# One inference step of a hybrid decoder on one core: store of new keys and values, pace of the sample group's keys, copies of new columns, scaling of the prompt's weights

## The chip, the cores and the metric

The kernel runs on one core of one Trainium2 chip. The metric is the device time of one execution in microseconds; the time before is 831.85 us, the median of three runs (829.95 to 833.71). Engines are named as in the profile: PE is the matmul engine, PEld its weight loads, DVE the vector engine, ACT the scalar engine, POOL the GpSimd engine, SP the engine whose queue issues most of the DMAs.

## The reference

One decoder layer with fp32 inputs is computed for two groups that share the weights: a prompt of 512 tokens, and a sample group of 8 sequences with 8 new tokens each and a cache of 1024 past keys and values. In outline:

```
h    = rmsnorm(x);  proj = h @ w_in                  # 1024 -> 3584 columns
rq, rk, rv, rg, aq, ak, av = split(proj)             # seven sections of 512: 8 heads x 64
ro   = silu(rg) * groupnorm(retention(rq, rk, rv))   # chunks of 128, recurrent state
ao   = dilated_attention(aq, concat(cache_k, ak), concat(cache_v, av))
                                                     # windows (128,1), (512,4), (2048,16), ALiBi
x    = x + concat(ro, ao) @ w_out
ua, ub = split(rmsnorm(x) @ w_up)
x    = x + (silu(conv3(ua)) * ub) @ w_down
y    = rmsnorm(x)
```

Outputs are y, the retention states, the windows of keys and values (the cache with the new rows behind it) and the last rows of the convolution, for both groups.

## The kernel before, in words

The 576 tokens lie along the free axis, the 128 columns of a weight chunk on the partitions. Every large product runs as three matmuls of split operands (high by high, high by low, low by high) over two halves of 288 tokens; the six matmuls for one block of 128 rows are one dense step (`dense`, L245 to L261). A chunk of `w_in` is eight steps. ACT and DVE split each chunk into its two parts (L219, L229), SP loads the chunks three deep (L211).

The work is written as Python generators, "streams", and a planner (`Merge`, L96 to L143) decides while the kernel is built in which order their instructions are emitted; on the chip each engine then runs its instructions in that order. A stream yields a cost, a delay before it may go on, and if wanted a third number, its charge (otherwise the cost is charged). Streams without a declared total (post-processing, a unit of attention) go first as soon as their delay is over. Among those with a total (`in_proj` 130,000 ns, `attn_prompt` 32,700, `attn_sample` 59,600) the one with the smallest sum of charge / what is left goes next. A stream that yields None is stuck until another moves on, and its sum is then lifted to the smallest of the others. `room(n)` sticks a stream while fewer than n of four PSUM tiles are free.

Heads are taken in pairs, hp 0 to 3. The input projection takes the three retention sections of each pair first, then for each pair the sections 5 (attention keys), 4 (queries) and 6 (values), then the gates. From pair 2 on it waits until `used` of the pair two before is 6: four prompt units and two sample units have done their value matmuls (L579). `in_post` (L521) scales the projected rows; for sections 5 and 6 it transposes them to token rows (`natural`, L489) and `store_window` (L501) writes them out: the prompt's 512 rows in one DMA, the sample group's 64 rows in eight, one for each sequence.

The prompt's attention runs in units of 128 queries (`attn_unit`, L741): score matmuls, penalties and minimum on DVE (L773), exponential on ACT (L780), reciprocal of the sums on DVE (L783), scaling of the weights of both heads on POOL (L785), then transposes on PE (L791), copies out of PSUM, and the value matmuls (L804).

The sample group's attention (`attn_sample`, L850) has eight units: pair hp and half g of the eight sequences. For each of a unit's four sequences x, `keys` (L870) transposes 768 gathered cache rows on PE (L877) and copies them into a key tile `kt` (L878; five buffers); then the loads of later keys and values are issued (L861, L863). When the four key tiles are there and the projection has given the pair's queries, new keys and new values, four POOL copies put the eight new key columns behind each tile's 768 (L977), and the unit itself is started: score matmuls (L887; columns 0 to 511, then 512 to 775), softmax (L894 to L904), transposes (L910), value matmuls (L923), transposes of the result (L938). At most two units are under way. After the first retention pass the three streams, projection, prompt and sample group, run side by side from 150 us on; the output projection follows at about 341 us, then the feed-forward part.

Of the kernel before, what the change touches and what calls it, by code (L numbers as in the profile page):

```python
# [14 lines left out]
OP = mybir.AluOpType  # L15
# [5 lines left out]
NP = 512  # L21
NS = 64
T = NP + NS
H2 = T // 2
B = 8
TS = 8
PAST = 1024
# [5 lines left out]
KEYS = 768  # L33
# [113 lines left out]
def decoder_step(ctx, tc, a):  # L147
    nc = tc.nc
    pe, dve, act, pool, sp = nc.tensor, nc.vector, nc.scalar, nc.gpsimd, nc.sync
# [7 lines left out]
    def mtile():  # L157
        return psm[0].tile([P, 512], F32, name="m", tag="m")
# [3 lines left out]
    def room(n):  # L162

        while held[0] + n > 4:
            yield None
        held[0] += n

    def give(n):
        held[0] -= n
# [4 lines left out]
    def f32(ap):  # L174
        return ap.bitcast(F32)
# [149 lines left out]
    def halves():  # L325
        return [(h2, slice(h2 * 64, h2 * 64 + 64)) for h2 in range(2)]
# [155 lines left out]
    for i in range(2):  # L482
        t = atp.tile([P, B, 32], F32, name=f"qb{i}", bufs=1)
# [17 lines left out]
    def store_window(nat, which, hp):  # L501
        c = slice(hp * P, (hp + 1) * P)
        op_ = a[f"o_w{which}_p"].rearrange("a (j p) h d -> p (a j) (h d)", p=P)[:, :, c]
        sp.dma_start(op_, nat[:, 0:4])
        os_ = a[f"o_w{which}_s"]
        for b in range(B):
            sp.dma_start(os_[b, PAST:PAST + TS].rearrange("t h d -> t (h d)")[:, c], nat[b * TS:(b + 1) * TS, 4])

    copies = []
    for which in "kv":  # L510
# [9 lines left out]
    R, A, ready, ret_done = {}, {}, set(), [0]  # L520
    def in_post(m, ps):  # L521
# [30 lines left out]
        else:  # L552
# [16 lines left out]
            if sec > 4:  # L569
                yield 0.0, 3100.0  # L570
                store_window(n, "k" if sec == 5 else "v", hp)
# [22 lines left out]
    for lst, shape, nme in ((sbds, [P, 3, P], "sbd"), (s0s, [P, B, P], "s0"), (qms, [P, B, NS], "qm")):  # L594
        t = rp.tile(shape, F32, name=nme, bufs=1)
# [4 lines left out]
    for i in range(2):  # L600
        t = rp.tile([P, 4, 10], F32, name=f"gst{i}", bufs=1)
# [134 lines left out]
    def load_bias(hp):  # L736
        for h2 in range(2):
            pbs[2 * hp + h2] = atp.tile([P, 512], F32, name="pb", tag="pb", bufs=2)
            sp.dma_start(pbs[2 * hp + h2], a["c_pbias"][2 * hp + h2])

    def attn_unit(hp, i):  # L741

        n = (i + 1) * P
        S, PT = [], []
        if i:

            q_ = A[hp][4][:, i * P:(i + 1) * P]
            qa = [kvb[0].tile([P, P], F32R, name=f"qa{h2}", tag=f"qa{h2}", bufs=2) for h2 in range(2)]
            ql = kvb[0].tile([P, P], F32R, name="ql", tag="ql", bufs=2)
            for h2, q in halves():  # L750
                act.copy(qa[h2][q], q_[q])
                act.copy(qa[h2][other(h2)], q_[q])
            yield 0.0, 1000.0
            for h2, q in halves():
                dve.tensor_sub(ql[q], q_[q], f32(qa[h2][q]))
            yield 0.0, 500.0
        yield from room(2)
        pss = [mtile() for _ in halves()]
        if i == 0:
            for h2, q in halves():  # L760
                pe.matmul(pss[h2][:, :n], A[hp][4][q, :P], A[hp][5][q, :n], start=True, stop=True)
        else:
            for h2 in range(2):
                pe.matmul(pss[h2][:, :n], qa[h2], kk[hp][h2][:, :n], start=True, stop=False)  # L764
            for h2, q in halves():
                pe.matmul(pss[h2][:, :n], ql[q], kk[hp][h2][q, :n], start=False, stop=True)  # L766
        for ps in pss:
            S.append((ps, atp.tile([P, 512], F32, name="s", tag="s", bufs=4),
                      atp.tile([P, 4], F32, name="sc", tag="sc", bufs=8)))
        scored[hp] = scored.get(hp, 0) + 1  # L770
        yield 2 * (i + 1) * 110.0, 100.0
        for h2, (ps, s, c) in enumerate(S):
            dve.tensor_tensor_reduce(out=s[:, :n], in0=ps[:, :n], in1=pbs[2 * hp + h2][:, 512 - n:], scale=1.0,  # L773
                                     scalar=3e38, op0=OP.add, op1=OP.min, accum_out=c[:, 0:1])
        give(2)
        if i == 3 and hp < 3:
            load_bias(hp + 1)
        yield 0.0, n + 300.0
        for ps, s, c in S:
            act.activation(s[:, :n], s[:, :n], AF.Exp, bias=c[:, 0:1], scale=-1.0, accum_out=c[:, 1:2])  # L780
        yield 0.0, 600.0
        for ps, s, c in S:
            dve.reciprocal(c[:, 2:3], c[:, 1:2])  # L783
        for ps, s, c in S:
            pool.tensor_scalar(s[:, :n], s[:, :n], c[:, 2:3], 1.0, op0=OP.mult, op1=OP.mult)  # L785
        yield 0.0, 2.5 * n + 300.0
        yield from room(2)
        for ps, s, c in S:
            ps = mtile()
            for j in range(i + 1):  # L790
                pe.transpose(ps[:, j * P:(j + 1) * P], s[:, j * P:(j + 1) * P], ident)  # L791
            PT.append((ps, atp.tile([P, 4, P], F32, name="pt", tag="pt", bufs=3)))
        yield 2 * (i + 1) * 110.0, 100.0
        for h2, (ps, pt) in enumerate(PT):
            (dve.tensor_copy if h2 else act.copy)(pt[:, :i + 1].rearrange("p j q -> p (j q)"), ps[:, :n])
        give(2)
        yield 0.0, n + 400.0
        if hp not in O:
            yield from room(1)
            O[hp] = [mtile(), 0]  # L800
        o_ps = O[hp][0]
        for j in range(i + 1):
            for h2, q in halves():
                pe.matmul(o_ps[q, i * P:(i + 1) * P], A[hp]["v"][:, j, q], PT[h2][1][:, j], start=j == 0, stop=j == i)  # L804
        yield (i + 1) * 230.0, 100.0
        used[hp] = used.get(hp, 0) + 1
        O[hp][1] += 1
        if O[hp][1] == 4:
            act.copy(aoT[:, hp, :NP], o_ps)
            give(1)  # L810
            half[hp] = half.get(hp, 0) + 1
            if half[hp] == 3:
                ready.add(4 + hp)
        flying["p"] -= 1
# [15 lines left out]
    def other(h2):  # L830
        return slice(64 - h2 * 64, 128 - h2 * 64)

    def attn_prompt():
        load_bias(0)
        for hp in range(4):
            while not (hp in A and all(x in A[hp] for x in (4, 5, 6))) or not kvb or hp and scored.get(hp - 1) != 4:
                yield None
            yield from k_split(hp)
            for i in range(4):
                while flying["p"] > 1:  # L840
                    yield None
                flying["p"] += 1
                mg.add(attn_unit(hp, i))
                yield 0.0, 2500.0, 2 * (i + 1) * 430.0
# [5 lines left out]
    def attn_sample():  # L850
        K, V, KT, SB = {}, {}, {}, {}
        units = [(hp, g) for hp in range(4) for g in range(2)]
# [17 lines left out]
        def keys(u, x):  # L870
            hp, g = units[u]
            b = 4 * g + x
            kt = kvb[0].tile([P, SK], F32, name="kt", tag="kt", bufs=5)
            for w in range(2):
                ps = mtile()
                for j in range(3):
                    pe.transpose(ps[:, j * P:(j + 1) * P], K[u, x][:, 3 * w + j], ident)  # L877
                (act.copy if w else dve.tensor_copy)(kt[:, w * 384:w * 384 + 384], ps[:, :384])  # L878
            del K[u, x]
            KT[u, x] = kt  # L880

        def unit(u):
            hp, g = units[u]
# [66 lines left out]
        def ahead(n, which):  # L950
            while loaded[which] < min(n, 32):
                u, x = divmod(loaded[which], 4)
                (K if which == "k" else V)[u, x] = load(u, x, which)
                loaded[which] += 1
# [7 lines left out]
        for u in range(8):  # L962
            hp, g = units[u]
            for x in range(4):
                yield from room(2)
                keys(u, x)
                give(2)
                yield 660.0, 1600.0
                ahead(4 * u + x + 4, "k")
                while len(V) > 5:  # L970
                    yield None
                ahead(4 * u + x + 1, "v")
            while not (hp in A and all(y in A[hp] for y in (4, 5, 6))) or flying["s"] > 1:
                yield None
            for x in range(4):
                b = 4 * g + x
                pool.tensor_copy(KT[u, x][:, KEYS:], A[hp][5][:, NP + b * TS:NP + (b + 1) * TS])  # L977
            flying["s"] += 1
            mg.add(unit(u), None, 600.0)
            yield 0.0, 1000.0, 4100.0  # L980

    last_in = []
    mg.add(in_proj(), 130.0e3)
# [6 lines left out]

    mg.add(ret_all())
    mg.add(attn_sample(), 59.6e3)
    mg.run(lambda: len(evac) == 3)
    psxx.close()
# [101 lines left out]
    for i in range(2):  # L1096
        u = fp.tile([P, UE], F32, name=f"ue{i}")
# [226 lines left out]
```

## Time and profile before

| | us |
|---|---|
| median of three runs (lowest, highest) | 831.85 (829.95, 833.71) |
| the profiled execution | 832.6 |
| its span, first to last instruction | 830.8 |
| PE busy | 813.8 |
| DVE busy | 412.5 |
| ACT busy | 295.3 |
| POOL busy | 148.0 |

The span is shorter than the execution's time, since start and end of the program lie outside of it. Matmuls are pipelined and their ends are modelled, so a busy PE can still be slower than its best. The granted clock is the share of full speed that PE's clock had.

### The profile page before, as it was taken

The numbers are of one execution on the slowest core, as the hardware profiler recorded it, in microseconds if no ns is written. First come the engines' busy times: TensorE is split into PE (matmuls) and PEld (weight loads), VectorE is DVE, ScalarE is ACT, GpSimd is POOL, SyncE is SP. The second block draws the span as 40 slices with busy tenths as digits, with TensorE's granted clock in tenths as the row PEclk, the third lists the DMA queues.
The fourth block names the chain that finished last, engine by engine and source line by source line (L and its number), as shares of the span: only waits on it lengthen the run. The fifth ranks groups of instructions, "written<-read, shape, count | busy, mean of one in ns | idle before, by whom it ended". The sixth has DMA issues, their size and how long they took to land.

```text
span 830.8 us, 15970 instructions
## 1 busy us (share of the span) xinstructions
PE 813.8 (98%) x6559; PEld 772.2 (93%) x6559; DVE 412.5 (50%) x792; ACT 295.3 (36%) x511; POOL 148.0 (18%) x234
## 2 busy tenths in 40 slices
PE   7999999999999999999999999999999999999995
PEld 6999999887887888999999999999999999999995
DVE  4664555665546456754545455432235545453333
ACT  5422232554446367333223323311223323342222
POOL 1321202011111113023122212100012322210111
PEclk9999999999999999999999999999999999999998
DMA  9354653658787774455265554543334445543213
GB/s 269 102 173 125 203 175 97 185 158 236 217 219 197 219 212 121 110 177 179 78 201 178 178 174 125 168 140 89 93 102 153 152 152 178 171 156 96 71 52 115
DMA packets 180247, 128.68 MB, mean 155 GB/s; under 512 B 15424, under 2 KB 176848, under 8 KB 179661
## 3 DMA queue, kind: packets, MB, share of 16 engines
q1 hardware_dynamic: 179021, 93.75, 40.3%
q10 hardware_dynamic: 928, 33.63, 11.2%
q8 instruction: 52, 0.85, 0.4%
q0 software_dynamic: 224, 0.28, 0.1%
q14 instruction: 22, 0.18, 0.1%
HBM read 121.52 MB, written 39.66 MB: 194 GB/s over the span
## 4 chain that ended last, share of the span: by engine, by line
PE 96%; ACT 1%; DVE 1%; DMA 0%; POOL 0%; issue 0%; ACTq 0%; DVEq 0%; POOLq 0%
PE d L254 75%; PE m L877 2%; PE m L923 2%; PE d L451 2%; PE m L804 1%; PE d L887 1%; PE m L791 1%; PE m L495 1%; PE px L410 1%; PE m L1214 1%; PE px L254 1%; PE m L663 1%; PE m L764 1%; PE d L910 1%; PE m L766 1%; PE m L627 1%
## 5 line engine op out<-in xcount | busy, mean ns | idle before, releaser
L219 ACT ACTIVATE whi<-wraw 128x1024 fp32r<-128x1024 f32 (+2 forms) x114 | 110.6, 970 | 364.9 <-issue 182.6
L229 DVE TENSOR_TENSOR wlo<-wraw,whi 128x1024 fp32r<-128x1024 f32 (+2 forms) x114 | 126.7, 1112 | 120.4 <-ACT whi L219 117.0
L254 PE MATMUL d<-bhi,whi 128*128 128x288 f32 x768 | 173.3, 307 | 0.0
L254 PE MATMUL d<-bhi,wlo 128*128 128x288 f32 x768 | 164.3, 295 | 0.0
L254 PE MATMUL d<-blo,whi 128*128 128x288 f32 x768 | 163.9, 295 | 0.0
L254 PE MATMUL d<-hhi,whi 128*128 128x288 f32 x704 | 150.9, 296 | 0.0
L254 PE MATMUL d<-hhi,wlo 128*128 128x288 f32 x704 | 150.8, 296 | 0.0
L254 PE MATMUL d<-hlo,whi 128*128 128x288 f32 x704 | 150.7, 296 | 0.0
L254 PEld LDWEIGHTS d<-bhi,whi 128*128 128x128 f32 x768 | 121.5, 189 | 5.2 <-issue 3.6
L254 PEld LDWEIGHTS d<-bhi,wlo 128*128 128x128 f32 x768 | 123.3, 188 | 0.0
L254 PEld LDWEIGHTS d<-blo,whi 128*128 128x128 f32 x768 | 123.2, 188 | 0.0
L254 PEld LDWEIGHTS d<-hhi,whi 128*128 128x128 f32 x704 | 113.4, 189 | 0.1
L254 PEld LDWEIGHTS d<-hhi,wlo 128*128 128x128 f32 x704 | 113.4, 189 | 0.0
L254 PEld LDWEIGHTS d<-hlo,whi 128*128 128x128 f32 x704 | 113.4, 189 | 0.0
L1122 DVE TENSOR_TENSOR ue<-d,rstd_b 128x512 f32<-128x512 f32 x22 | 15.2, 691 | 74.6 <-PE d L254 74.6
L1141 POOL TENSOR_TENSOR g<-g,cv 128x512 f32<-128x512 f32 x20 | 25.7, 1287 | 142.1 <-DVE g L1138 136.7
L785 POOL TENSOR_SCALAR s<-s,sc 128x128 f32<-128x128 f32 (+3 forms) x32 | 18.2, 575 | 141.1 <-DVE sc L783 139.9
L1038 POOL TENSOR_TENSOR acc<-acc,sq 128x576 f32<-128x576 f32 x13 | 20.9, 1607 | 104.2 <-ACT sq L1037 104.2
L1127 POOL COPY cout<-ue 128x2 f32<-128x2 f32 x22 | 5.7, 258 | 137.8 <-DVE ue L1122 137.8
L878 DVE COPY kt<-m 128x384 f32<-128x384 f32 x32 | 17.8, 556 | 22.4 <-PE m L877 21.2
L878 ACT COPY kt<-m 128x384 f32<-128x384 f32 x32 | 15.3, 477 | 38.4 <-PE m L877 36.8
L877 PE MATMUL m<-ident,kc 128*128 128x128 f32 x192 | 27.2, 277 | 0.9 <-ACT spt L916 0.9
(264 smaller groups left out, 1030.7 us busy)
## 6 DMA issues: line engine op xcount, KB each, us to landing
wraw<-in_w_up_dram SPq DMA_DIRECT2D x44, 512.0 KB
wraw<-in_w_in_dram SPq DMA_DIRECT2D x26, 512.0 KB
kc<-in_cache_win_k_dram SPq DMA_DIRECT2D x32, 256.0 KB
vc<-in_cache_win_v_dram SPq DMA_DIRECT2D x32, 256.0 KB
wraw<-in_w_down_dram SPq DMA_DIRECT2D x16, 384.0 KB
wraw<-in_w_down_dram SPq DMA_DIRECT2D x16, 320.0 KB
kc<-in_cache_win_k_dram SPq DMA_DIRECT2D x64, 64.0 KB
vc<-in_cache_win_v_dram SPq DMA_DIRECT2D x64, 64.0 KB
```

The lines of the kernel that those rows point to most:

```text
L219: act.activation(split[i][0][:, c], raw[i][:, c], AF.Copy)
L229: dve.tensor_sub(lo[:, c], raw[i][:, c], f32(hi[:, c]))
L254: pe.matmul(ps[:, C0 + s * H2:C0 + (s + 1) * H2], wt[:, rows[k] if rows else k - k0], x[k][:, s * H2:(s + 1) * H2], start=first and k == k ...
L410: pe.transpose(ps[:, s], xn[:r, j, k * P:(k + 1) * P], ident[:r, :r])
L451: pe.matmul(ps[i][:, C0 + s * H2:C0 + (s + 1) * H2], wt[:, k], x[k][:, s * H2:(s + 1) * H2], start=k == 0 and wt is hi and x is xhis, stop ...
L785: pool.tensor_scalar(s[:, :n], s[:, :n], c[:, 2:3], 1.0, op0=OP.mult, op1=OP.mult)
L877: pe.transpose(ps[:, j * P:(j + 1) * P], K[u, x][:, 3 * w + j], ident)
L878: (act.copy if w else dve.tensor_copy)(kt[:, w * 384:w * 384 + 384], ps[:, :384])
L923: pe.matmul(ps[x * 32:(x + 1) * 32, :P], pt[:n, j, x * 32:(x + 1) * 32], v, start=j == 0, stop=j == 6, tile_position=(0, x * 32))
L1038: pool.tensor_tensor(acc, acc, sq, op=OP.add)
L1122: dve.tensor_mul(u[:, 2:NP + 2], ya[:, :NP], rstd_b[:, :NP])
L1141: eng.tensor_tensor(g[:, :NP], g[:, :NP], c[:, :NP], op=OP.mult)
```

## The change

Four edits. `store_window` writes the sample group's 64 new rows in one DMA. The scaling of the prompt's weights puts the first head of a pair on POOL and the second on DVE, and the planned delay behind it goes from 2.5 n + 300 to 1.25 n + 500 ns. `attn_sample` charges 1685 ns after each key tile, where it charged 660 after each and 4100 after a unit's start. The new key columns are copied right after each key tile if the projection has made them, and at the unit's start otherwise.

```diff
         os_ = a[f"o_w{which}_s"]
-        for b in range(B):
-            sp.dma_start(os_[b, PAST:PAST + TS].rearrange("t h d -> t (h d)")[:, c], nat[b * TS:(b + 1) * TS, 4])
+        sp.dma_start(os_[:, PAST:PAST + TS].rearrange("b t h d -> b t (h d)")[:, :, c], nat[:NS, 4])
@@ attn_unit
-        for ps, s, c in S:
-            pool.tensor_scalar(s[:, :n], s[:, :n], c[:, 2:3], 1.0, op0=OP.mult, op1=OP.mult)
-        yield 0.0, 2.5 * n + 300.0
+        for eng, (ps, s, c) in zip((pool, dve), S):
+            eng.tensor_scalar(s[:, :n], s[:, :n], c[:, 2:3], 1.0, op0=OP.mult, op1=OP.mult)
+        yield 0.0, 1.25 * n + 500.0
@@ attn_sample, keys
             KT[u, x] = kt
+            if hp in A and 5 in A[hp]:
+                new_keys(u, x)
+
+        early = set()
+
+        def new_keys(u, x):
+            hp, g = units[u]
+            b = 4 * g + x
+            if (u, x) not in early:
+                early.add((u, x))
+                pool.tensor_copy(KT[u, x][:, KEYS:], A[hp][5][:, NP + b * TS:NP + (b + 1) * TS])
@@ attn_sample, main loop
                 keys(u, x)
                 give(2)
-                yield 660.0, 1600.0
+                yield 660.0, 1600.0, 1685.0
                 ahead(4 * u + x + 4, "k")
...
             for x in range(4):
-                b = 4 * g + x
-                pool.tensor_copy(KT[u, x][:, KEYS:], A[hp][5][:, NP + b * TS:NP + (b + 1) * TS])
+                new_keys(u, x)
             flying["s"] += 1
             mg.add(unit(u), None, 600.0)
-            yield 0.0, 1000.0, 4100.0
+            yield 0.0, 1000.0
```

## Rows read from the trace of the kernel before

**Rows 1.** The page: span, busy time of each engine, chain that ended last.
```profile
span 830.8 us, 15970 instructions
PE 813.8 (98%) x6559; PEld 772.2 (93%) x6559; DVE 412.5 (50%) x792; ACT 295.3 (36%) x511; POOL 148.0 (18%) x234
...
PE 96%; ACT 1%; DVE 1%; DMA 0%; POOL 0%; issue 0%; ACTq 0%; DVEq 0%; POOLq 0%
```

**Rows 2.** Windows: length, then busy us (instructions) by engine, clock, DMA share, GB/s.
```profile
core 0: us, PE busy (x) PEld busy (x) DVE busy (x) ACT busy (x) POOL busy (x), PEclk, DMA share, GB/s
195.00:200.00 5.00, 3.70 (x36) 2.87 (x38) 2.00 (x5) 2.72 (x7) 0.00 (x0) 0.93 0.91 259
200.00:205.00 5.00, 4.63 (x64) 3.66 (x55) 2.83 (x10) 2.69 (x8) 1.25 (x6) 0.73 0.80 231
...
150.00:341.00 191.00, 188.26 (x1829) 159.25 (x1828) 111.36 (x284) 102.63 (x248) 29.75 (x73) 0.99 0.69 192
```

**Rows 3.** Timeline of PE around the gate: start us, us, engine, line, operation.
```profile
188.37 1.51 PE L887 MATMUL d<-kt,qb 128*32 128x512 f32 x16
189.81 1.09 PE L804 MATMUL m<-pt,n 128*64 128x128 f32 x16
...
195.38 0.71 PE L495 MATMUL m<-ident,t 128*128 128x128 f32 x5
...
199.21 2.76 PE L923 MATMUL m<-vc,spt 128*32 128x128 f32 x48
...
203.99 0.51 PE L254 MATMUL d<-bhi,whi 128*128 128x288 f32 x2
```

**Rows 4.** Chain of waits in order of time: start us, us, piece.
```profile
199.28 3.27 PE m L923 x56
...
244.38 1.80 PE m L923 x56
...
247.54 0.79 PE d L254 x6
```

**Rows 5.** Waits from 140 to 340 us: waiter, releaser: total us, times, longest.
```profile
PEld m L791 <- POOL s L785: 1.8, 7, 0.4
PEld d L887 <- POOL kt L977: 1.8, 3, 1.2
```

**Rows 6.** Line L507, SP's stores: count, duration ns min/median/max, first and last.
```profile
L507 SPq DMA_DIRECT2D out_dram<-n x64: 276/294/713, 137.3 to 304.9; - x64
```

**Rows 7.** Timeline of all engines at the start of unit 3.
```profile
232.38 1.06 PE L887 MATMUL d<-kt,qb 128*32 128x512 f32 x8
232.39 1.23 DVE L229 TENSOR_TENSOR wlo<-wraw,whi 128x1024 fp32r<-128x1024 f32 x1
232.40 1.64 POOL L977 COPY kt<-t 128x8 f32<-128x8 f32 x4
...
233.72 1.01 PE L887 MATMUL d<-kt,qb 128*32 128x264 f32 x8 [0.27 <-POOL kt L977]
...
234.65 1.09 PE L791 MATMUL m<-ident,s 128*128 128x128 f32 x8
```

**Rows 8.** Groups by line and shape, 150 to 345 us: busy us, mean ns.
```profile
L785 POOL TENSOR_SCALAR s<-s,sc 128x512 f32<-128x512 f32 x8 | 5.5, 692 | 30.4 <-DVE sc L783 30.4
...
L902 DVE TENSOR_SCALAR ss<-ss,ssc 128x776 f32<-128x776 f32 x8 | 5.2, 651 | 0.3
```

**Rows 9.** Timeline of POOL and DVE at 170.8 us.
```profile
170.79 1.24 POOL L785 TENSOR_SCALAR s<-s,sc 128x256 f32<-128x256 f32 x2 [7.77 <-DVE sc L783]
170.85 0.83 DVE L902 TENSOR_SCALAR ss<-ss,ssc 128x776 f32<-128x776 f32 x1
```

**Rows 10.** Windows of the dense steps (line L254) between unit 1's keys and launch.
```profile
core 0: us, PE busy (x), PEclk, DMA share, GB/s
170.20:173.10 2.90, 1.26 (x8) 1.00 0.72 208
173.10:181.60 8.50, 2.96 (x18) 1.00 0.55 154
181.60:184.80 3.20, 2.59 (x20) 1.00 0.75 219
184.80:188.30 3.50, 2.12 (x14) 1.00 0.87 253
```

## The prediction

> **What bounds the kernel now.** I read the page's busy shares and chain of waits first. PE is busy for 98% of the span and the chain that ended last is 96% PE [rows 1]: what matters is only what PE waits for, or what makes it slower. DVE, ACT, POOL and the queues have slack, so a microsecond saved on them counts only where PE is late for it.
>
> Next I cut the span by windows. All that the change touches runs from 150 to 341 us (attention, beside the input projection). There PE is busy for 188.26 of 191 us, 2.74 idle. Of these, 1.30 + 0.37 = 1.67 us lie between 195 and 205, and only there is the granted clock down, at 0.93 and 0.73 [rows 2] (1.00 is 2.4 GHz, a half 1.2 GHz: part of the stretch ran at the lower level). PE's timeline shows why: between 195.38 and 203.99 no dense step is issued, only attention work with gaps, and the projection's steps return at 203.99 [rows 3]. This is the gate in in_proj: for pair 2 it waits until used[0] is 6, that is until unit 1 of the sample group (pair 0, second half), launched at 188.37, has done its value matmuls (199.21 and after). The clock costs something besides the idle: the 56 value matmuls took 3.27 us there and 1.80 us in unit 3 [rows 4], 1.47 us more. So the gate costs 1.67 + 1.47 = 3.1 us. What PE's weight loads waited for in the stage is small: 1.8 us for POOL's copies of new columns, 1.8 us for POOL's scaling, never over 1.2 us at once [rows 5]. The most that these rows let the change win is thus about 3.1 + 1.8 + 1.8 = 6.7 us, 0.8%.
>
> **The change part by part.**
>
> *One store for eight.* 64 issues of some 0.29 us or more on SP become 8 [rows 6]; the bytes and 512 byte runs stay. SP issues weight and cache loads in between, up to 3.5 us earlier then; but no wait of PE on a load of weights stands in the stage's list, three weight chunks and three key tiles are in flight, so cover is there and the term is 0 (bounds: 0.4 us gained, the same lost if the single store blocks the queue longer).
>
> *New columns copied at once.* The same 32 POOL copies are made, but after each key tile and not four in a row before the unit's score matmuls. Where the late copies hurt is seen at unit 3: its matmuls over the first 512 columns start at 232.38, those that need the new columns only at 233.72, and the next PE work at 234.65, 2.27 us for a unit that takes 1.44 us at 188.37 to 189.81 (the same 16 matmuls, 1.51 us by their row) [rows 3, 7]. That is 0.83 us, and it should go. The other waits of this kind, 1.8 - 1.17 = 0.6 us, overlap with matmuls still running; I count 0.3. For the first half of each pair the copy still waits for the projection's new keys, as now. A copy that is queued early blocks POOL's scaling behind it only until the key tile's buffer is free, and PE has by then read it in its own order. Term: -1.1 us (bounds 0 and -1.8).
>
> *Scaling on two engines.* Two POOL instructions of 0.69 us at 512 columns follow each other today [rows 8]; one of them goes to DVE. DVE's tensor_scalar over 776 columns takes 0.65 us on average [rows 8], so 512 columns are an estimated 0.65 x 512 / 776 = 0.43 us. The pair then takes max(0.69, 0.43) instead of 1.38, at best 0.69 us less for the widest of four blocks; the written delay before the transposes shrinks by 1580 - 1140 = 0.44 us of it, so most of the gain goes into an earlier place in the order, not into a shorter wait. The total wait to be had is 1.8 us in seven pieces of at most 0.4 [rows 5]; half is 0.9, and half of that reaches PE, whose matmuls are queued ahead: -0.45 us. DVE gets 16 x about 0.3 = 5 us more in a stage where it is busy for 111 of 191 us [rows 2]; behind each on its queue stand key copies and weight splits that PE meets later. Bounds: -1.8, and +0.9 if DVE is late instead.
> The two engines do not run freely beside each other: at 170.8 a DVE scaling of 776 columns took 0.83 us, not 0.65, while POOL's pair of 256 columns took 1.24 us [rows 9], and a POOL copy stood for over a microsecond while DVE subtracted two SBUF tensors [rows 7]. The Trainium skill, SBUF — State Buffer, section "Who interferes with whom", says that the port pair shared by VectorE and GpSimd is an exclusive lock, and that a tensor_scalar in a two-port mode takes it. By that rule the two scalings would run one after the other, 0.69 + 0.43 = 1.12 us, and the gain in latency would be 0.26 us, below the 0.44 that the order gives away; by free running it is 0.69. The row lies between (each longer, neither doubled).
>
> *Even pace.* The planner takes the stream with the smallest sum of p / left. A unit's charge is 4 x 660 + 4100 = 6740 before and 4 x 1685 = 6740 after, so the stream's overall share is unchanged; what moves is where in a unit the keys and the launch fall. I worked it out for unit 1, on which the gate hangs. When its first key comes, the sample stream has 59,600 - 6,740 = 52,860 left, the projection about 130,000 - 108 x 738 = 50,300 (15 chunks of 8 steps, 120, are done at the gate; 9 lie between this key and the launch and about 3 behind it). One dense step is worth 738 / 50,300 = 0.0147. A key charge was 660 / 52,860 = 0.0125, one step; now it is 0.032, and the sums for the second, third and fourth key and the launch, 0.032, 0.065, 0.099 and 0.134, are passed after 3, 5, 7 and 9 dense steps. The trace of before has 1, 3, 3 and 2 steps (matmul counts over six, those cut by a window's edge left out) between the same points [rows 10]: 1, 4, 7 and 9. So today the keys are already spread, by PSUM tiles that are not free and by the written delays, and the new pace asks for nearly the same places. The launch comes 0 to 1 step later (its 0.6 us delay comes on top); a step is 0.79 us [rows 4]. One of unit 2's keys then falls behind the gate instead of ahead, 0.8 us of filler. Term: +0.8 us for the launch, about -0.3 for that filler: +0.5 us. Bounds: -3.1 (the gate's whole price gone) and +5.6 (below). Unit 3 and the second gate (projection's pair 3) get a launch at 9 steps after unit 2's by the same working and end at 246, with the next dense step at 247.54 [rows 4], no idle time; later units wait for the projection itself (pairs 2 and 3), which the pace doesn't move.
>
> **Sum.** 0 - 1.1 - 0.45 + 0.5 = about -1.1 us. The profiled execution took 832.6 us (830.8 span and 1.8 around it), 0.75 above the median of the three runs; on the median that is 831.85 - 1.1 = 830.7 us.
>
> **The rivals.**
> *B, the gate closes:* unit 1 is launched two or three steps earlier against the projection, because its keys no longer meet the prompt's PSUM tiles, and its chain ends with dense work still there. For it: the 8.5 us between two keys of unit 1, three dense steps and otherwise attention work [rows 10], is a collision that another order can miss. Against: the pace alone holds the launch to 9 steps. Time: -3.1 - 1.1 - 0.45 = -4.65, 827.2 us.
> *C, the gate opens wider, slower:* a key that is due later finds fewer than two free PSUM tiles (a stuck stream loses its credit) and falls into such a hole. Price: 8.5 instead of 3.2 us between two keys [rows 10], 5.3, less 1.2 for two keys as filler, plus a second 1.47 for work at the lower clock: +5.6 us, less the direct gains of 1.55: +4.05, 835.9 us; at the second gate, where no idle time but no cover either is seen, as much could come again. It decides from the point where unit 1's score matmuls stand behind the projection's last step before the gate; today about three steps lie behind them.
> *D, the scalings lock each other out and delay DVE's queue:* -1.1 + 0.5 + 0.2 (a quarter of the +0.9 above), 831.4 us. The row at 170.8 shows part of it; by the rule of SBUF — State Buffer in the Trainium skill, cited above, it is the likely form of that edit.
>
> **How the numbers follow.** Forecast 0.52 (own range 828 to 834), B 0.22, C 0.18, D 0.08. What a measurement of this kernel can tell is about 0.5%, 4.2 us: below 827.7 is faster, above 836.0 slower. Faster: most of B, 0.18, and 0.04 of the forecast's edge, 0.22. Slower: C is centred on the line and open upwards, 0.12, with 0.04 from orders that I did not foresee: 0.16. Same: 0.62. The range reaches B's lower half and C's middle: 826.3 to 837.0.
>
> **What would show it.** Right: a stretch without dense steps before unit 1's value matmuls end remains, near 195 us, 8 to 10 us long, with idle of 1.5 to 2.5 us and a lower clock; unit 1's score matmuls at 188 to 190 us; every unit's 16 score matmuls take 1.44 us; eight store issues. Wrong: no lower clock between 150 and 341 us (B); PE idle there above 5 us or a second stretch at a lower clock (C); POOL's and DVE's scalings each longer by the other's time (D).

## The result, and the profile after

The changed kernel takes 840.21 us (median of 6 runs, 838.01 to 841.32), beside 831.56 us of the kernel before on the same chip (6 runs, 829.95 to 833.71). The ratio is 1.0098, with an interval of 1.0078 to 1.0117: 8.65 us slower. The forecast was 830.7 us and its range ended at 837.0. The prediction was wrong, in its sign and in its range.

The page of the changed kernel, to be held against [rows 1]. This execution took 838.01 us, the lowest of its runs, so the trace shows the loss at its lowest; where the longer executions spend some 2 us more, no trace shows.

```profile
span 836.2 us, 15865 instructions
...
PE 812.0 (97%) x6559; PEld 770.5 (92%) x6559; DVE 416.9 (50%) x808; ACT 295.4 (35%) x511; POOL 140.6 (17%) x218
```

PE is still the bound, and now it has more holes. The same windows as in [rows 2] (us; PE, PEld, DVE, ACT and POOL busy with counts; granted clock; DMA share; GB/s):

```profile
195.00:200.00 5.00, 3.02 (x57) 2.17 (x59) 3.85 (x13) 3.21 (x11) 0.51 (x2) 1.00 0.86 262
200.00:205.00 5.00, 5.00 (x53) 4.00 (x45) 2.71 (x8) 2.61 (x7) 0.00 (x0) 1.00 0.57 165
150.00:341.00 191.00, 181.54 (x1780) 152.50 (x1778) 110.07 (x289) 100.47 (x242) 21.62 (x53) 0.99 0.68 192
```

PE is idle for 191 - 181.54 = 9.46 us of this stage, where it was 2.74: 6.7 us more. The start of the sample stage shifts by some us from execution to execution, so I take the time from unit 0's score matmuls to the end of the span as a second measure: 667.2 us before, 673.9 after, again 6.7. So the loss of this execution is idle PE in the attention stage. It is not at the gate alone; by tens of microseconds (same columns, changed kernel):

```profile
190.00:200.00 10.00, 7.58 (x98) 5.84 (x94) 7.48 (x21) 5.91 (x16) 0.82 (x4) 1.00 0.88 253
210.00:220.00 10.00, 7.56 (x61) 6.51 (x60) 6.25 (x17) 5.54 (x15) 1.01 (x3) 1.00 0.89 249
230.00:240.00 10.00, 8.71 (x80) 6.98 (x79) 5.11 (x10) 3.91 (x7) 1.58 (x8) 1.00 0.84 257
280.00:290.00 10.00, 7.92 (x49) 7.03 (x47) 5.57 (x14) 4.46 (x12) 1.36 (x4) 0.83 0.63 184
```

These four hold 2.42 + 2.44 + 1.29 + 2.08 = 8.23 of the 9.46 us. At the gate, where the clock had been down in [rows 2], it stayed at 1.00; it fell instead from 280 to 290, around the hole at 283 (0.83: part of that stretch ran at 1.2 GHz), where nothing had been idle before.

PE's waits there (waiter, releaser: total us, times, longest). The longest of the kernel before ([rows 5] has its weight loads):

```profile
PE m L877 <- ACT spt L916: 0.9, 1, 0.9
```

and those over 1 us of the changed kernel:

```profile
PE m L876 <- DVE sc L772: 2.4, 2, 2.1
PE d L254 <- ACT spt L926: 1.5, 1, 1.5
PE d L254 <- DVE ssc L904: 1.3, 1, 1.3
PE m L790 <- POOL s L784: 1.1, 1, 1.1
```

Each of the long waits occurs once, and they lie on four different pairs of lines: key transposes that wait for the prompt's penalties, dense steps that wait for what a unit does after its scores, prompt transposes that wait for the scaling. Three of the four name an instruction of DVE or ACT that empties a PSUM tile, none a load. The largest, by the timeline of all engines (start, us, instruction, idle before it):

```profile
279.19 0.94 ACT L909 ACTIVATE ss<-ss,ssc 128x776 f32<-128x776 f32 x1
280.13 1.04 ACT L219 ACTIVATE whi<-wraw 128x1024 fp32r<-128x1024 f32 x1
...
281.20 1.23 DVE L229 TENSOR_TENSOR wlo<-wraw,whi 128x1024 fp32r<-128x1024 f32 x1 [1.67 <-ACT whi L219]
282.54 0.62 DVE L912 TENSOR_SCALAR ss<-ss,ssc 128x776 f32<-128x776 f32 x1
283.34 0.68 DVE L772 CUSTOM_DVE_ANT_0 s<-m,pb 128x512 f32<-128x512 f32 x1
284.08 0.90 PE L876 MATMUL m<-ident,kc 128*128 128x128 f32 x3 [2.08 <-DVE sc L772]
```

Read it from the bottom: PE's key transposes need the tile that L772 frees; L772 stands on DVE behind L912, that behind the weight split L229, and L229 waited 1.67 us for ACT's half of the split, which stood behind a unit's exponential. Nothing here is long, but each engine takes its queue in order, and a key now falls where a unit, a prompt block and a weight split meet. The second wait is of the same kind on other buffers: the dense products and a unit's transposes share two PSUM tiles (`psd`).

```profile
216.38 0.56 DVE L877 COPY kt<-m 128x384 f32<-128x384 f32 x1 [0.26 <-PE m L876]
216.86 0.55 DVE L924 COPY spt<-d 128x384 f32<-128x384 f32 x1
...
217.87 0.26 ACT L926 COPY spt<-d 64x128 f32<-64x128 f32 x1
218.18 0.53 PE L254 MATMUL d<-bhi,whi 128*128 128x288 f32 x2 [1.50 <-ACT spt L926]
```

The key copy L877 goes ahead of L924 on DVE, L926 frees the tile last, and a projection chunk waits for it. The third is alike: a key copy stands ahead of L904, which frees the tile of a unit's scores, and the next dense step, at 235.44, waits 1.29 us for it.

```profile
233.86 0.56 DVE L877 COPY kt<-m 128x384 f32<-128x384 f32 x1 [1.23 <-PE m L876]
234.33 0.95 DVE L904 CUSTOM_DVE_ANT_0 ss<-d,sb 128x776 f32<-128x776 f32 x1
```

What the planner did with unit 1, by the windows of the dense steps between its keys and its launch (as [rows 10]: us, PE and PEld busy, granted clock, DMA share, GB/s; six matmuls are a step, and the odd ones are of steps that a window's edge cuts):

```profile
168.90:174.50 5.60, 3.08 (x20) 2.46 (x18) 1.00 0.96 266
174.50:180.80 6.30, 1.79 (x14) 1.58 (x12) 1.00 0.19 53
180.80:184.90 4.10, 2.95 (x20) 2.48 (x19) 1.00 0.86 261
184.90:189.20 4.30, 2.93 (x20) 2.45 (x18) 1.00 0.76 221
```

That is 3, 2, 3 and 3 steps, keys at 3, 5 and 8 and a launch at 11 dense steps after the first key; 3, 5, 7 and 9, and up to one more, were forecast. PE's timeline at the gate, beside [rows 3]:

```profile
189.28 1.51 PE L897 MATMUL d<-kt,qb 128*32 128x512 f32 x16
...
192.22 0.82 PE L876 MATMUL m<-ident,kc 128*128 128x128 f32 x6
...
197.00 1.08 PE L933 MATMUL m<-vc,spt 128*32 128x128 f32 x32 [0.86 <-ACT ka L824]
...
201.79 0.40 PE L254 MATMUL d<-bhi,whi 128*128 128x288 f32 x1
```

Unit 1 is launched at 189.28 (188.37 before), and no dense step runs from 192.22 to 201.79. So the gate is where I had put it, and the loss is elsewhere too.

### The profile page after: what moved, and what is told of

Read it like the earlier page. It is cut to its first block, busy times and chain, and to the rows that moved or that the text cites. A ratio compares the mean times of both kernels' runs of the same rounds, so it can differ in the third digit from the quotient of the medians.

```text
span 836.2 us, 15865 instructions
## 1 busy us (share of the span) xinstructions
PE 812.0 (97%) x6559; PEld 770.5 (92%) x6559; DVE 416.9 (50%) x808; ACT 295.4 (35%) x511; POOL 140.6 (17%) x218
## 4 chain that ended last, share of the span: by engine, by line
PE 92%; ACT 2%; DVE 2%; DMA 1%; issue 1%; POOL 0%; SPq 0%; ACTq 0%; DVEq 0%; POOLq 0%
PE d L254 74%; PE m L876 2%; PE m L933 2%; PE d L897 1%; PE m L803 1%; PE d L451 1%; PE m L790 1%; PE m L495 1%; PE m L1223 1%; DMA wraw<-in_w_in_dram 1%; PE px L254 1%; PE m L662 1%; PE m L763 1%; DMA xn<-in_x_prompt_dram 1%; PE d L920 1%
## 5 line engine op out<-in xcount | busy, mean ns | idle before, releaser
L229 DVE TENSOR_TENSOR wlo<-wraw,whi 128x1024 fp32r<-128x1024 f32 (+2 forms) x114 | 126.7, 1112 | 123.5 <-ACT whi L219 120.6
L254 PE MATMUL d<-bhi,whi 128*128 128x288 f32 x768 | 173.1, 307 | 2.8 <-ACT spt L926 1.5
L254 PE MATMUL d<-bhi,wlo 128*128 128x288 f32 x768 | 164.5, 296 | 0.0
L254 PE MATMUL d<-blo,whi 128*128 128x288 f32 x768 | 164.2, 295 | 0.0
L254 PE MATMUL d<-hhi,whi 128*128 128x288 f32 x704 | 150.9, 296 | 0.0
L254 PE MATMUL d<-hlo,whi 128*128 128x288 f32 x704 | 150.8, 296 | 0.0
L254 PE MATMUL d<-hhi,wlo 128*128 128x288 f32 x704 | 150.7, 296 | 0.0
L254 PEld LDWEIGHTS d<-bhi,whi 128*128 128x128 f32 x768 | 121.8, 189 | 8.2 <-issue 4.6
L254 PEld LDWEIGHTS d<-bhi,wlo 128*128 128x128 f32 x768 | 123.6, 189 | 0.0
L254 PEld LDWEIGHTS d<-blo,whi 128*128 128x128 f32 x768 | 123.4, 189 | 0.0
L254 PEld LDWEIGHTS d<-hhi,whi 128*128 128x128 f32 x704 | 113.5, 189 | 0.1
L254 PEld LDWEIGHTS d<-hhi,wlo 128*128 128x128 f32 x704 | 113.5, 189 | 0.0
L254 PEld LDWEIGHTS d<-hlo,whi 128*128 128x128 f32 x704 | 113.5, 189 | 0.0
L877 ACT COPY kt<-m 128x384 f32<-128x384 f32 x32 | 15.3, 477 | 49.8 <-PE m L876 49.5
L877 DVE COPY kt<-m 128x384 f32<-128x384 f32 x32 | 17.8, 555 | 28.3 <-PE m L876 28.3
L876 PEld LDWEIGHTS m<-ident,kc 128*128 128x128 f32 x192 | 21.8, 142 | 6.7 <-DVE sc L772 3.0
```

The source lines that it names most:

```text
L229: dve.tensor_sub(lo[:, c], raw[i][:, c], f32(hi[:, c]))
L254: pe.matmul(ps[:, C0 + s * H2:C0 + (s + 1) * H2], wt[:, rows[k] if rows else k - k0], x[k][:, s * H2:(s + 1) * H2], start=first and k == k ...
```

## The experiments

Ratios are against the kernel before on the same chip, with their 95% interval; microseconds worked out from a ratio are its part of 831.6. The four edits are the store, the early copies, the scaling (the second engine with its shorter planned delay) and the pace.

**First round: which edit.** Four kernels: store and copies, scaling alone, pace alone, all but the pace.

```diff
# a1: of the change, only
+        sp.dma_start(os_[:, PAST:PAST + TS].rearrange("b t h d -> b t (h d)")[:, :, c], nat[:NS, 4])
+            if hp in A and 5 in A[hp]:
+                new_keys(u, x)
# a2: of the change, only
+        for eng, (ps, s, c) in zip((pool, dve), S):
+            eng.tensor_scalar(s[:, :n], s[:, :n], c[:, 2:3], 1.0, op0=OP.mult, op1=OP.mult)
+        yield 0.0, 1.25 * n + 500.0
# a3: of the change, only
+                yield 660.0, 1600.0, 1685.0
+            yield 0.0, 1000.0
# a4: the change, but
-                yield 660.0, 1600.0, 1685.0
+                yield 660.0, 1600.0
-            yield 0.0, 1000.0
+            yield 0.0, 1000.0, 4100.0
```

> The single store and the early copies alone, on the kernel before. Neither has a planned cost or delay, so PE, DVE and ACT get the same instructions in the same order as before; only SP's and POOL's lists differ. All theories: between 0 and -1.8 us against before (the 0.83 us at unit 3 goes). If it were slower by 2 us or more, the loss of the whole change would be one of transfers or of POOL's queue.

> The scaling on two engines with its shorter planned delay alone, on the kernel before. Theory O (the new pace puts the sample group's launches where they collide with chunk changes and DVE's queue): -1 to +1 us. Theory V (the scaling on DVE, sharing its way to SBUF with POOL, delays everything behind it on DVE): +5 to +9 us. Theory S (any new order of the streams makes its own collisions, no edit in particular): +3 to +6 us.

> The even pace alone, on the kernel before. Theory O: +6 to +9 us, nearly all of the change's +8.65. Theory V: 0 to +1 us. Theory S: +3 to +6 us, with waits at other places than in the changed kernel.

> The changed kernel with the old pace (store, copies and scaling stay). Theory O: -2 to 0 us against before. Theory V: +4 to +8 us. Theory S: +2 to +5 us, that is a2 less about 1.

Measured: a1 829.25 us, 0.997 (0.9959 to 0.998); a2 838.23, 1.0072 (1.0057 to 1.0087); a3 837.76, 1.0063 (1.0048 to 1.0078); a4 830.62, 0.9981 (0.9971 to 0.9991). The pace makes the whole loss: without it the change gains 1.6 us, with it it loses 8.1, and alone it loses 5.2. None of the three theories fits all of it: a4 came out as O had it, a3 as S in its time, a2 where V and S meet, and a1 gained more than the 1.8 us that it was given. Rival B's mechanism shows in a4, where the gate nearly closes: unit 1 is launched 6 dense steps after its first key (9 before, 11 in the change), and from the start of the last dense matmul ahead of the gate to that of the next one it is 4.4 us (10.3 before, 9.8 in the change). The same four stretches have little idle time and the full clock.

```profile
190.00:200.00 10.00, 9.80 (x121) 8.81 (x121) 5.17 (x11) 4.40 (x11) 0.00 (x0) 1.00 0.87 244
210.00:220.00 10.00, 9.69 (x121) 8.30 (x120) 6.28 (x19) 5.15 (x13) 1.21 (x4) 1.00 0.87 234
230.00:240.00 10.00, 9.73 (x128) 8.78 (x127) 5.08 (x11) 4.40 (x11) 1.62 (x6) 1.00 0.81 235
280.00:290.00 10.00, 10.00 (x129) 8.98 (x128) 4.24 (x9) 3.96 (x10) 1.00 (x4) 1.00 0.87 249
```

A surprise stood beside it. The scaling alone loses 6.0 us, and together with a1's two edits it loses nothing. The three parts happen to add up (-2.5 + 6.0 + 5.2 = 8.7, the change 8.1), but a2's loss is not in the changed kernel: PE waits in a2 for loads of keys, 5.1 us in all, and the changed kernel's waits have no load among them.

```profile
PE m L877 <- DMA kc<-in_cache_win_k_dram: 5.1, 3, 2.9
```

**Second round: what saves the scaling, and which units the pace hurts.** b1 is the scaling with the single store, b2 the scaling with the early copies and the eight stores; b3 has all of the change with the even pace in units 0 and 1 only, b4 from unit 2 on only.

```diff
# b3
+                yield 660.0, 1600.0, 1685.0 if u < 2 else 660.0
+            yield 0.0, 1000.0, 0.0 if u < 2 else 4100.0
# b4
+                yield 660.0, 1600.0, 660.0 if u < 2 else 1685.0
+            yield 0.0, 1000.0, 4100.0 if u < 2 else 0.0
```

> The scaling on two engines and the single store, old pace, late copies. PE, DVE and ACT have the same order as in a2 (838.2) and a4 (830.6); the three differ on SP and POOL alone. Theory Q (in this order the eight stores hold the key loads behind them on SP's queue: in a2 PE waited 5.1 us for key tiles' DMAs): 830 to 833 us. Theory K (the late copies hold the units up): 836 to 838 us.

> The scaling on two engines and the early copies, old pace, eight stores: the other half of what parts a2 from a4. Theory Q: 836 to 838 us, with PE waiting for key loads as in a2. Theory K: 830 to 833 us.

> The changed kernel, but the even pace only in units 0 and 1, the old charges (660 and 4100) from unit 2 on. Theory G (the pace costs at the first gate: unit 1 is launched 14 dense steps after unit 0 in the changed kernel, 8.8 in a4 with the old pace, and the projection is stuck meanwhile): 834 to 838 us, a stretch without dense steps near 195 us. Theory L (it costs later, where launches meet chunk changes and DVE's queue at 215, 233 and 283 us): 830 to 832 us.

> The changed kernel, but the old charges in units 0 and 1 and the even pace from unit 2 on. Theory G: 830 to 834 us, no stretch without dense steps near 195 us. Theory L: 835 to 839 us, with waits of over 1 us between 210 and 290 us.

Measured: b1 830.27, 0.9966 (0.9952 to 0.9979); b2 840.07, 1.008 (1.0049 to 1.0111), 2 us above what theory Q gave it. The store decides. b1 and a2 have the same order of instructions on PE, DVE and ACT, as have a4 and b2; what differs is one store for eight, and that is worth 1.0072 - 0.9966 = 0.0106, 8.8 us, in the one pair and 0.0099, 8.2 us, in the other. SP's queue shows how (start, time from the first to the last of a group, instruction). In a2:

```profile
233.24 4.74 SPq L507 DMA_DIRECT2D out_dram<-n  x8
238.08 0.84 SPq L739 DMA_DIRECT2D pb<-in_c_pbias_dram  x2
239.02 0.38 SPq L861 DMA_DIRECT2D kc<-in_cache_win_k_dram  x1
```

and in b1:

```profile
228.02 0.68 SPq L506 DMA_DIRECT2D out_dram<-n  x1
229.20 0.95 SPq L738 DMA_DIRECT2D pb<-in_c_pbias_dram  x2
230.24 0.51 SPq L860 DMA_DIRECT2D kc<-in_cache_win_k_dram  x1
```

The eight issues hold SP for 4.74 us ahead of the key load, the single one for 0.68; PE's key transposes in a2 then start at 243.34, after 2.90 us of idle for that load. In all PE waits 8.0 us for key loads in b2, and for none in a4 and b1. In the order of before these eight stores cost PE no wait for a load; in the order of the scaling they cost 8 us.

b3 834.75, 1.002 (1.0006 to 1.0035); b4 835.79, 1.0046 (1.0028 to 1.0063). Against a4 that is 0.0039 and 0.0065, 3.2 and 5.4 us, 8.6 together, near the 9.7 us between a4 and the change. Both halves lose, each where its pace is even, so theory G was right for b3 and theory L for b4: b3's idle time is for the most part at the gate, b4's lies from 210 on, the largest piece at 283. Windows 190 to 200 and 280 to 290 of b3,

```profile
190.00:200.00 10.00, 7.22 (x86) 5.46 (x78) 7.36 (x20) 5.57 (x14) 0.82 (x4) 1.00 0.88 250
280.00:290.00 10.00, 9.63 (x124) 8.66 (x125) 3.79 (x8) 3.44 (x9) 0.91 (x5) 1.00 0.64 180
```

and of b4:

```profile
190.00:200.00 10.00, 9.81 (x120) 8.97 (x121) 4.66 (x10) 3.90 (x9) 0.00 (x0) 1.00 0.86 248
280.00:290.00 10.00, 7.91 (x91) 7.15 (x93) 5.77 (x15) 3.55 (x9) 1.35 (x4) 0.83 0.67 192
```

So it is not one gate that opened wider.

**Third round: how much pace, the second engine, and one wait.** c1 and c2 charge 1000 and 1345 for a key and the rest of 6740 at the end of the unit; c3 is a1 with the second engine but the old delay, so that its PE order is that of a1; c4 is the change with DVE's weight split of the projection put into DVE's queue two dense steps later, PE's, ACT's, POOL's and SP's order unchanged.

```diff
# c1
+                yield 660.0, 1600.0, 1000.0
+            yield 0.0, 1000.0, 2740.0
# c2
+                yield 660.0, 1600.0, 1345.0
+            yield 0.0, 1000.0, 1360.0
# c3: a1, and
+        for eng, (ps, s, c) in zip((pool, dve), S):
+            eng.tensor_scalar(s[:, :n], s[:, :n], c[:, 2:3], 1.0, op0=OP.mult, op1=OP.mult)
         yield 0.0, 2.5 * n + 300.0
# c4: the change, and
-            if k == k0 + 1:
+            if k == k0 + (3 if key[0] == "in" else 1):
```

> The changed kernel with 1000 charged after each key and 2740 after the unit's start (same sum, 6740; the changed kernel has 1685 and 0, a4 has 660 and 4100). Theory O (the more of the charge lies between the keys, the later the launches and the more it costs): 831 to 833 us, between a4 (830.6) and the changed kernel (840.2), nearer to a4. Theory S (each order has its own collisions, without a trend): anywhere from 830 to 840 us.

> The changed kernel with 1345 after each key and 1360 after the unit's start. Theory O: 834 to 837 us, above c1 and below the changed kernel. Theory S: anywhere from 830 to 840 us, above the changed kernel or below c1 as well.

> a1 (single store, early copies, old pace) with the scaling on two engines, but the old planned delay behind it (2.5 n + 300): PE and ACT have a1's order exactly, and DVE gets the 16 scalings more. What the second engine is worth by itself. If DVE has room: -1 to 0 us against a1 (829.3). If DVE's queue or the shared way to SBUF hurts: +1 to +3 us.

> The changed kernel, but in the input projection DVE's split of the next weight chunk is written two dense steps later. PE, ACT, POOL and SP keep the changed kernel's order exactly; on DVE the split moves behind the softmax work that at 280 us stood behind it (the split waited 1.67 us for ACT, and PE then 2.08 us for DVE's reduction of the prompt's scores). If that place is the head of DVE's queue: 836 to 838 us, and the wait of PE at 283 us is gone. If DVE is late there for its load and not for that order: 839 to 841 us.

Measured: c1 831.28, 0.9992 (0.9982 to 1.0002); c2 832.09, 1.0003 (0.9992 to 1.0014). With a4 and the change, charges of 660, 1000, 1345 and 1685 a key give 830.6, 831.3, 832.1 and 840.2 us: the loss rises with the charge, but nearly all of it comes in the last step. c1 is where theory O had put it, c2 is 2 us below. A smooth price for each step of spread is refuted; an order is discrete, and the last one meets the collisions.

c3 830.8, 0.9984 (0.9971 to 0.9997): 1.2 us above a1 by the ratios, with overlapping intervals. The second engine by itself wins nothing that shows; whether it costs a microsecond is not settled.

c4 838.7, 1.0077 (1.0056 to 1.0099), between the two ranges that were given. At the place of the 2.1 us wait, in c4:

```profile
283.51 1.02 PE L876 MATMUL m<-ident,kc 128*128 128x128 f32 x6
...
284.92 1.22 DVE L229 TENSOR_TENSOR wlo<-wraw,whi 128x1024 fp32r<-128x1024 f32 x1
```

The key transposes no longer wait, and PE is busy for 9.74 of the 10 us from 280 to 290 at clock 1.00 (7.92 at 0.83 in the change). From unit 0 to the end the execution is 2.1 us shorter; the medians differ by 1.5, with overlapping intervals. That the queue behind the weight split made this wait is shown by the trace; that the wait's end reaches the total is likely, and not beyond the noise.

**Fourth round: spread keys, or a late launch?** d1 spreads the first three keys as the change does and lets the launch come soon after the fourth; d2 leaves the keys where they were and makes the launch late.

```diff
# d1
+                yield 660.0, 1600.0, 1685.0 if x < 3 else 660.0
+            yield 0.0, 1000.0, 1025.0
# d2
+                yield 660.0, 1600.0, 660.0 if x < 3 else 4760.0
+            yield 0.0, 1000.0, 0.0
```

> The changed kernel with 1685 after a unit's first three keys, 660 after the fourth and 1025 after the launch (same sum, 6740): keys spread as in the changed kernel, the launch right after the last key as before. If the late launch is what costs: 831 to 834 us. If the spread keys cost (they fall among other work that holds DVE and ACT): 837 to 841 us.

> The changed kernel with 660 after the first three keys, 4760 after the fourth and none after the launch: keys bunched as before, the launch as late as in the changed kernel or later. If the late launch is what costs: 837 to 842 us. If the spread keys cost: 830 to 834 us.

Measured: d1 841.49, 1.0093 (1.0065 to 1.0121); d2 833.05, 0.9999 (0.9978 to 1.002). Spread keys cost as much with an early launch as with the late one, and a late launch with close keys costs nothing that shows. That the two cost the same is in part chance: d1 has its other large wait, 2.4 us for the scaling at 204.21, at the gate, where the change waits 1.1. So what I had argued about, the place of the launch, is not what costs; the places of the keys are. That is not spread as such: unit 1's keys come 3, 5 and 8 dense steps after its first in the change and in d1, but also 1, 3 and 6 after it in c2 and 1, 4 and 7 in c3, and these two lose nothing that shows.

What the losing orders share is the largest wait of the changed kernel. Every run that charges 1685 between the keys from unit 2 on has it once, 9.8 us after unit 5's launch: the change (284.08), and a3, b4 and d1, shown in this order (a3 has the lines of before, one number higher here). Only c4, which moves the weight split, does not.

```profile
285.58 0.55 PE L877 MATMUL m<-ident,kc 128*128 128x128 f32 x3 [2.09 <-DVE sc L773]
282.39 0.55 PE L876 MATMUL m<-ident,kc 128*128 128x128 f32 x3 [2.09 <-DVE sc L772]
289.74 0.55 PE L876 MATMUL m<-ident,kc 128*128 128x128 f32 x3 [2.08 <-DVE sc L772]
```

In all other runs no single wait of the key transposes for that instruction is over 0.6 us, and in most it is 0.3 or none.

No run is better than a1 and b1, which beat the kernel before by 2.5 and 2.8 us: the single store with either the early copies or the scaling. a4, all three, gains 1.6, and the three intervals overlap.

## Why the prediction was wrong, step by step

**The pace, +0.5: the step that failed.** The planner's arithmetic held for unit 1, the only unit that I worked out: 3, 5, 8 and 11 dense steps for 3, 5, 7 and 9 or 10. So did the place of the gate, and unit 1's launch within 1 us. The price failed. I counted the launch at the gate and one key as filler, and nothing for what a key brings along: six transposes that need two PSUM tiles of the pool that the prompt uses too, and a copy of 384 columns on each of DVE and ACT. Measured against a4 the term is +9.7 us, and alone +5.2.

Two sentences carried the low price. "The new pace asks for nearly the same places" is true of unit 1 with the pace alone: in a3 its keys and its launch come after 2, 4, 7 and 9 dense steps, where before had 1, 4, 7 and 9. It is not true in the order that the scaling's shorter delay makes, a term that I had priced by itself: in a4 they come after 1, 2, 2 and 6, so that the pace moves them by two to six steps. And "later units wait for the projection itself (pairs 2 and 3), which the pace doesn't move" is refuted by b4, where from unit 2 on the pace costs 5.4 us, more than in units 0 and 1, and by a3, which keeps unit 1's places and loses far behind it: from unit 5's launch to unit 6's it takes 25.75 us, and before took 21.53. The signs of being right that I had named, but for the lower clock, came out; they looked at unit 1, the gate, the score matmuls and the stores, and not where the loss was.

**The store, 0.** My reason, that no wait on a load stood in the list, was true of the order of before and not of the order that the scaling makes. There the store is worth 8 us (a2 with b1, b2 with a4). It does not change the sum's sign, but the bounds of 0.4 us either way were far too narrow: they were read from the old order, and the change makes a new one. The issues are as foreseen, beside [rows 6] (count; ns min, median, max; first and last start):

```profile
L506 SPq DMA_DIRECT2D out_dram<-n x8: 671/677/748, 136.1 to 301.3; - x8
```

That is 0.67 to 0.75 us on SP's queue, from the first to the last issue of a pair's section, for what took 2.78 to 4.68 before, and 4.74 at the place above.

**The early copies, -1.1: right at its place.** Unit 3's scores and the next PE work, beside [rows 7]:

```profile
231.83 1.51 PE L897 MATMUL d<-kt,qb 128*32 128x512 f32 x16
233.27 0.88 PE L876 MATMUL m<-ident,kc 128*128 128x128 f32 x6
```

1.44 us for the unit, 2.27 before. a1 has the same (232.62 to 234.07) and gains 2.5 us in all, store and copies not told apart. The other place where its profiled execution is shorter is the gate: 16.66 us from unit 1's launch to unit 2's, 18.84 before, with the same order on PE. There a1's clock stayed at 1.00, beside 0.93 and 0.73 in [rows 2]. With the scaling in place the copies win nothing (b1 without them, a4 with them).

**The scaling, -0.45.** Most of the gain was to come from an earlier place in the order, and the earlier place does come, as rival B: in a4 and b1 the gate is nearly closed. I had put B down to the pace and against it that "the pace alone holds the launch to 9 steps"; it is the shorter delay that closes the gate, and the pace that opens it again. a4 and b1 are 1.6 and 2.8 us faster, B's price was 4.65 with the copies. But closing the gate wins nothing that shows: c3, with the old delay and 8.0 us between dense matmuls at the gate, takes 830.8 us, and a4 830.6. As a gain to be had, the gate's 3.1 us were too many. 1.47 us of them were the lower clock, and that was probably not in the median: the profiled execution of before had a mean clock of 0.994, and of 25 others beside c1 to c4, 24 had 0.996 or more. There is no second trace of before to show it.

**The rivals.** C had the right sign and one of its marks, PE idle above 5 us; its price of +4 us, and that "as much could come again" at the second gate, make 8 us, near the measured 8.65 by luck. Its mechanism, a key that falls into the gate's hole for want of a PSUM tile, is at most b3's half (3.2 us), and the gate did not open wider than before (9.8 us between dense matmuls, 10.3 before); what the trace shows of the other half are waits on DVE's and ACT's queues and on the two dense tiles, far from the first gate. D had no share in it that a run shows: c3 lies within 1.2 us of a1. The mark of a lower clock near 195 failed as well; in the profiled execution the clock fell around 283 us.

**What stays open.** Why the last step of the charge (1345 to 1685) costs four to five times what the two before it cost together, and which of the collisions c2 escapes: the runs show that the loss jumps and that the 2.1 us wait comes with it, not how the planner gets from one order to the other. How far the other waits (1.5, 1.3 and 1.1 us) add up to the rest was not tried one by one, as c4 did for the largest.

## What to carry to other kernels

Where a planner writes out the order of the queues, an edit of a weight or of a delay is an edit of the whole order behind it, and its cost can't be bounded by the waits of the old order: price what each moved item takes with it (tiles, evacuations, loads), on every in-order queue that it joins, and for every unit and not for one. A transfer that costs nothing in one order can be worth 1% in the next, so try the parts of a change singly and in pairs before the sum of their effects is believed. Small stores on the queue that also issues the loads are worth joining into one even where no wait shows yet.

## What the runs showed of the hardware

DVE and POOL scale beside each other at a price, but not one after the other. Two places of the changed kernel, by the timeline:

```profile
229.37 0.70 POOL L784 TENSOR_SCALAR s<-s,sc 128x512 f32<-128x512 f32 x1 [13.20 <-DVE sc L782]
...
287.24 0.49 DVE L784 TENSOR_SCALAR s<-s,sc 128x512 f32<-128x512 f32 x1
287.24 0.97 POOL L784 TENSOR_SCALAR s<-s,sc 128x512 f32<-128x512 f32 x1 [7.35 <-DVE sc L782]
```

Started together at 287.24, DVE takes 0.49 us (0.43 was estimated) and POOL 0.97, where POOL, almost alone at 229.37, takes 0.70: 0.27 longer. The pair is done in 0.97 us there, and in 1.06 at 229.37, where DVE started 0.57 us later, behind its second reciprocal (L782); it took 1.38 before.

What the 0.27 us are can be read from the other widths of the same line. DVE takes, at the shortest, 0.29, 0.35, 0.42 and 0.49 us for 128, 256, 384 and 512 columns: 0.067 us for each 128 columns, and some 0.22 us that do not grow with them (the 0.43 left these out by going in proportion). The part that grows is 0.13, 0.20 and 0.27 us at 256, 384 and 512 columns. POOL beside a DVE scaling that starts with it or up to 0.1 us earlier is longer by 0.13 (0.61 for 0.48), 0.21 (0.80 for 0.59) and 0.27 us. The Trainium skill, SBUF — State Buffer, section "Who interferes with whom", calls the shared port pair an exclusive lock; the rows agree with a lock that lasts for the part of DVE's instruction that grows with its columns, and not for all of its 0.49 us, as the prediction's 1.12 us for the pair had it.
